# Norm gains spread by TensorE instead of loaded, two weight slabs outside the ring, and a rare path's loads on another queue, in a two-layer encoder with 32 experts

## The chip, the cores and the metric

One Trainium2 chip; the kernel runs on one of its cores. The metric is device time in microseconds (us), the median of several runs. Five engines work side by side, each from its own list of instructions: TensorE (PE; its weight loads stand in the profile as PEld), VectorE (DVE), ScalarE (ACT), GpSimd (POOL) and SyncE (SP). They wait for each other, and for transfers, on semaphores. Transfers (DMA) are issued from an engine's list and then run by themselves.

## What is computed

256 tokens of 1024 numbers pass two layers. In each, a mixer (pooling, a recurrent scan in two directions, attention) is followed by a norm, and this by a mixture of 32 experts and a second norm:

```python
x = layer_norm(DEEPNORM_ALPHA * x + y, ln1_g[l], ln1_b[l])      # y: the mixer's output
...
x = layer_norm(DEEPNORM_ALPHA * x + m, ln2_g[l], ln2_b[l])      # m: the experts' output
...
def layer_norm(x, g, b):
    xf = x.astype(jnp.float32)
    mu = jnp.mean(xf, -1, keepdims=True)
    var = jnp.mean(jnp.square(xf - mu), -1, keepdims=True)
    return ((xf - mu) * lax.rsqrt(var + LN_EPS) * g + b).astype(x.dtype)
...
    def expert_block(args):
        xb, e = args
        h = jax.nn.silu(xb @ w_gate[e]) * (xb @ w_up[e])
        return h @ w_down[e]
```

Each token goes to two experts of one group of eight; gain and bias of each norm are rows of 1024 numbers.

## The kernel before, in words

**Weights.** The experts' weights of a layer are 192 slabs of 128x2048 fp32 (1 MB each), in an order that the host lays out: 8 groups (NQ) of 4 experts, and of each group 8 slabs for gate, 8 for up, 8 for down. SP loads them in this order into a ring of 22 slabs (`slab()`, `RING`, `FLIGHT`); the name of the tile is `w`, that of the source `in_e_w`. The generator `loads` (line 1036) issues one load each time it is advanced (line 1039). 22 are issued ahead of the first group, while the mixer's end and the routing still run. Then `w(n)` takes the oldest slab and issues the next load, which waits until the matmuls of the slab that lay in its place are done. SP's loads go over eight lanes, each with a semaphore (DMAHW0 to DMAHW7), so that eight are out at a time and a ninth waits for the first of them.

**A group.** `experts` loops over the groups q. `gate_up` runs matmuls of gate (`pg`), then up (`pu`), a slab at a time; `between(n)` puts other work behind slab n. `hid_t` transposes the hidden rows (`pht`), `down` runs slabs 16 to 23 (`py`), ACT copies the result (`y`), and `combine` multiplies it with the one-hot matrix that scatters rows back to tokens (`pc`), which DVE adds to `xr`. The rows of the next group are gathered with a one-hot matrix `OH` by matmuls (`xg`); ACT and DVE apply gain and bias of the norm to them from columns (`lnc`), with the channel on the partition. A gathered place holds CH = 32 rows an expert.

**The norm rows.** The residual `xr` needs gain and bias along the row, the same on every partition. `ln_load` (line 1027) loads them with four broadcast transfers of 128x512 (256 KB each, line 1031): ahead of group 0 for the first norm, and after group 6 for the second. With the first, `gates` computes `xr` from the normed x in group 0 (lines 1177 to 1179): eight DVE instructions of 128x512, then two on ACT for the factor alpha. With the second, the layer's last norm is done. In the last layer `scaled` (lines 1440 to 1453) divides it between DVE and POOL, in unequal parts of the columns, and four transfers store the result.

**A path that is not taken.** Behind group 1 (`OVQ`) `overflow` (line 1303) tests whether an expert got more than 32 rows. All engines read the count (line 1304) and branch (line 1305); with these inputs the path is not taken. Within it weights are loaded once more, a quarter slab at a time (`ow`), from ACT's queue (line 1317).

**Order of the work.** The instructions stand on each engine in the order in which the code issues them. SBUF buffers of tag "r" (`s2`, nine of 128x512) and `x8` (two of 128x2x1024: one holds x, the other `x1T`, the transposed tokens for the router, and then `xr`) and eight PSUM banks (tag "r" five, `bank`; tag "c" three, `bankc`) are given out in that order too.

Of the kernel before, what the change touches and what calls it, by code (L numbers as in the profile page):

```python
# [22 lines left out]
NQ = NE // 4  # L23
ALPHA = float((2 * DEPTH) ** 0.25)
# [29 lines left out]
START = 9  # L54
OVQ = 1
FLIGHT = 22
LN_COLS0 = 704
LN_COLS = 832
VARIANT = [0, 1, 1, 0]
LOX = [0, 0, 0, 0]  # L60
PRE = 2
# [5 lines left out]

@with_exitstack
def tile_encoder(ctx: ExitStack, tc: tile.TileContext, x_tok, x_t, w_a0, w_a1, w_b0, w_b1, w_o,
                 cols, ln_rows, consts, rcnt, e_w, out):  # L70
    nc = tc.nc
    V, A, G, PE = nc.vector, nc.scalar, nc.gpsimd, nc.tensor
    PSUM = bass.MemoryType.PSUM
# [8 lines left out]
    def x8(name):  # L82
        return xp.tile([128, 2, D], F32, name=name, tag="x8", bufs=2)
# [16 lines left out]
    def slab(dt=F32):  # L100
        return wp.tile([128, 2048], dt, name="w", tag="w", bufs=RING)
# [30 lines left out]
    P = load_cols(0, E)  # L132
# [3 lines left out]
    x = x8("x")  # L136
# [3 lines left out]
    ident = kc[:, K_ID:K_ID + 128]  # L140
# [17 lines left out]
    slot = cp.tile([128, 2, NE], F32, name="slot")  # L158
# [3 lines left out]
    lnc = cp.tile([128, 392], F32, name="lnc")  # L162
# [46 lines left out]
    def s2(shape, name):  # L209
        return mp.tile(shape, F32, name=name, tag="r", bufs=RB)  # L210
# [812 lines left out]

        return [lambda i=i: put(i, 0, fin[0][i]) for i in range(2)], [second(i) for i in range(2)]

    def ln_load(l, n, one=False):
        gb = []
        t_ = slab() if one else None
        for m in range(4):
            b = t_[:, 512 * m:512 * m + 512] if one else s2([128, 512], "lnr")  # L1030
            nc.sync.dma_start(out=b, in_=ln_rows[l, n + m // 2:n + m // 2 + 1, 512 * (m % 2):512 * (m % 2) + 512].to_broadcast([128, 512]))
            gb.append(b)
        return gb

    def loads(l):
        for q in range(NQ):
            for n in range(24):
                t_ = slab()
                nc.sync.dma_start(out=t_, in_=e_w[l, q, n])
                yield t_.rearrange("p (a n) -> p a n", a=4)  # L1040

    def route_all(l, xh, wo_tail):
        gb = ln_load(l, 0)


        mask = tiny([128, 2, NE], "mask")
        iota32 = iota[:, 0:32]
# [1 line left out]
        xk = [xh[:, i].rearrange("p (c k) -> p k c", k=8) for i in range(2)]  # L1049
# [87 lines left out]
        mv0 = ln_rstd(st[0])  # L1137
# [8 lines left out]
        mv1 = ln_rstd(st[1])  # L1146
# [16 lines left out]
        xr = x8("xr")  # L1163

        def exps():
            next(r0)
# [2 lines left out]
        def gates():  # L1169
            for r in (r0, r1):  # L1170
                for _ in r:
                    pass
            yield
            for i in range(2):
                for h in range(2):
                    sl = (slice(None), i, slice(512 * h, 512 * h + 512))
                    V.tensor_tensor(xr[sl], xh[sl], gb[h], op=OP.mult)
                    V.tensor_tensor(xr[sl], xr[sl], gb[2 + h], op=OP.add)
                A.mul(xr[:, i], xr[:, i], ALPHA)

        def count():
            cm = tiny([128, 1], "cm")
# [3 lines left out]
            V.tensor_reduce(cnf, pcm[0:1, 0:128], axis=AX.X, op=OP.max)  # L1186
            V.tensor_copy(cnt, cnf)

        return xr, (oh0, banks), exps, gates, count

    def gather_half(ps, x1k, oh, i):
        for k in range(8):
# [16 lines left out]
    def experts(l, x1, xr, oh0, exps, gates, count, wts, feed):  # L1209

        x1k = x1.rearrange("p i (c k) -> p i k c", k=8)

# [27 lines left out]
        def gated(oh, gts):  # L1240
            V.tensor_tensor(oh, oh, gts.rearrange("p i (a s) -> p i a s", s=1).to_broadcast([128, 2, 4, CH]), op=OP.mult)
# [101 lines left out]
        xg = []  # L1343
        late_half(0)
        oh, done = oh0[0], None
        for q in range(NQ):
            def w(n):
                t_ = wts.pop(0)
                wts.extend(v_ for v_ in (next(feed, None),) if v_ is not None)
                return lambda a: t_[:, a]  # L1350

            more = q + 1 < NQ
            cut_ = q == OVQ
            if q:
                gated(oh, four(gate, q))
            nxt, oht, steps = [None], [], None

            def step(n):
                for _ in range(n):
                    nxt[0] = next(steps, nxt[0])  # L1360

            def between(n):
                nonlocal steps
                if q == 0 and n == 1:
                    late_half(1)
                    exps()
                    A.preload_act_table_set(SETS_SILU)
                    more_ = gates()
                    next(more_)
# [43 lines left out]
            if cut_:  # L1413
# [23 lines left out]
        mv0 = ln_rstd(st[0])  # L1437
        put(1, 1)
        if last:
            def scaled(i, mv, n):  # L1440
                for e, lo, hi in ((V, 0, n), (G, n, 1024)):
                    if e is G:
                        o_ = xr[:, i, lo:hi]
                        G.tensor_scalar(o_, o_, mv[:, 0:1], mv[:, 3:4], op0=OP.subtract, op1=OP.mult)  # L1444
                        G.tensor_tensor(o_, o_, gb[1][:, lo - 512:hi - 512], op=OP.mult)  # L1445
                        G.tensor_tensor(o_, o_, gb[3][:, lo - 512:hi - 512], op=OP.add)  # L1446
                    else:
                        for m, (c, op0, op1) in enumerate(((0, OP.subtract, OP.mult), (3, OP.mult, OP.add))):
# [53 lines left out]
    resid = iter(())  # L1502
    for l in range(DEPTH):
        wo_tail = mixer(l, P, x, *slabs[:2], *block, resid)
        feed = loads(l)
        wts = [next(feed) for _ in range(FLIGHT)]
        xr, oh0, exps, gates, count = route_all(l, x, wo_tail)
        x, slabs, P, block, resid = experts(l, x, xr, oh0, exps, gates, count, wts, feed)
# [43 lines left out]
def _layout(inp):  # L1552
# [7 lines left out]
    rw = 256  # L1560
# [52 lines left out]
    d["ln_rows"] = np.ascontiguousarray(np.stack([g["ln1_g"], g["ln1_b"], g["ln2_g"], g["ln2_b"]], 1))  # L1613
# [23 lines left out]
```

## Time and profile before

| | |
|---|---|
| median of 3 runs | 1278.93 us (1277.48 to 1283.57) |
| the profiled execution | 1281.9 us, its span 1280.1 us |
| mean granted TensorE clock | 0.871 of full speed |
| busy share of the span | PE 77%, DVE 26%, ACT 19%, POOL 7% |
| bytes moved | 438.67 MB, 343 GB/s over the span |
| chain that ended last | 24% loads of w from in_e_w, all else 1% and less |

Slices of equal length across the page tell where the stretches lie: the mixers are those in which little is moved (37 GB/s in the third slice, 9 GB/s in the 22nd), the experts those in which some 420 GB/s are moved. The experts of the first layer run from about 181 to 626 us, those of the second from about 821 to 1264 us. A share of busy time is an average over these; what an edit is worth has to be read in its stretch.

### The profile page before, as it was taken

The numbers are of one execution on the slowest core, as the hardware profiler recorded it, in microseconds if no ns is written. First come the engines' busy times: TensorE is split into PE (matmuls) and PEld (weight loads), VectorE is DVE, ScalarE is ACT, GpSimd is POOL, SyncE is SP. The second block draws the span as 40 slices with busy tenths as digits, with TensorE's granted clock in tenths as the row PEclk, the third lists the DMA queues.
The fourth block names the chain that finished last, engine by engine and source line by source line (L and its number), as shares of the span: only waits on it lengthen the run. The fifth ranks groups of instructions, "written<-read, shape, count | busy, mean of one in ns | idle before, by whom it ended". The sixth has DMA issues, their size and how long they took to land. (4 is left out here: it accounts for less than half of the span.)

```text
span 1280.1 us, 18020 instructions
## 1 busy us (share of the span) xinstructions
PE 985.9 (77%) x7571; PEld 480.6 (38%) x7571; DVE 335.9 (26%) x774; ACT 239.2 (19%) x554; POOL 94.0 (7%) x137
## 2 busy tenths in 40 slices
PE   8988998933997777776698979989239977777753
PEld 7755763220441212221286657632214422223100
DVE  5937632110100001010368286411001000010103
ACT  5326422001110101010252353220011101010000
POOL 1143000000000000000101451000000000000002
PEclk9979999965998888886799789999669988888887
DMA  9413789998999999999940227999989999999994
GB/s 373 165 37 131 307 327 418 420 418 331 420 419 419 420 420 420 420 419 420 417 170 9 89 79 320 365 420 420 419 330 420 419 420 420 419 420 420 419 420 188
DMA packets 63452, 438.67 MB, mean 343 GB/s; under 512 B 7040, under 2 KB 7296, under 8 KB 11520
## 3 DMA queue, kind: packets, MB, share of 16 engines
q1 hardware_dynamic: 62784, 436.61, 83.1%
q8 instruction: 64, 1.05, 0.3%
q10 hardware_dynamic: 576, 0.79, 0.2%
q14 instruction: 28, 0.23, 0.0%
HBM read 436.32 MB, written 1.05 MB: 342 GB/s over the span
## 5 line engine op out<-in xcount | busy, mean ns | idle before, releaser
L172 PE MATMUL pg<-w,xg 128*32 128x512 f32 x1024 | 143.4, 658 | 120.3 <-ACT xg L1230 73.1
L172 PE MATMUL pu<-w,xg 128*32 128x512 f32 x1024 | 157.0, 700 | 39.2 <-DMA w<-in_e_w_dram 39.1
L172 PE MATMUL py<-w,hT 128*32 128x512 f32 x1024 | 146.0, 697 | 53.4 <-DMA w<-in_e_w_dram 42.4
L1261 DVE TENSOR_TENSOR h<-h,pu 128x512 f32<-128x512 f32 x16 | 11.0, 688 | 422.5 <-PE pu L172 218.3
L172 PEld LDWEIGHTS pg<-w,xg 128*32 128x32 f32 x1024 | 25.3, 114 | 215.8 <-DMA w<-in_e_w_dram 87.2
L1230 ACT ACTIVATE xg<-xg,lnc 128x128 f32<-128x128 f32 x112 | 41.8, 457 | 326.5 <-PE xg L168 219.6
L1293 DVE TENSOR_TENSOR xr<-xr,pc 128x512 f32<-128x512 f32 x56 | 38.5, 688 | 242.2 <-PE pc L172 242.2
L168 PEld LDWEIGHTS xg<-OH,xr 128*128 128x128 f32 x256 | 65.0, 331 | 61.9 <-issue 55.5
L168 PEld LDWEIGHTS xg<-OH,x 128*128 128x128 f32 x256 | 65.0, 331 | 59.4 <-issue 53.0
L172 PEld LDWEIGHTS py<-w,hT 128*32 128x32 f32 x1024 | 29.1, 117 | 154.1 <-DMA w<-in_e_w_dram 83.4
L168 PE MATMUL xg<-OH,xr 128*128 128x128 f32 x256 | 75.7, 433 | 12.0 <-DVE OH L1201 4.0
L168 PE MATMUL xg<-OH,x 128*128 128x128 f32 x256 | 75.6, 429 | 11.0 <-PEq L1305 4.1
L172 PE MATMUL pc<-y,OHT 128*128 128x512 f32 x128 | 70.0, 641 | 1.4 <-ACT y L1285 1.4
L1285 ACT COPY y<-py 128x512 f32<-128x512 f32 x32 | 18.7, 585 | 242.8 <-PE py L172 242.8
L231 POOL TENSOR_TENSOR w<-w 128x512 fp32r<-128x512 f32 (+1 forms) x20 | 25.2, 1265 | 497.4 <-ACT w L230 497.4
L172 PEld LDWEIGHTS pu<-w,xg 128*32 128x32 f32 x1024 | 23.6, 116 | 97.7 <-DMA w<-in_e_w_dram 80.5
L269 PE MATMUL wo<-w 128*128 128x512 f32 x192 | 46.5, 398 | 0.0
L196 POOL TENSOR_TENSOR lnmv<-lnmv,eps 128x1 f32<-128x1 f32 x8 | 4.8, 602 | 524.5 <-DVE lnmv L195 524.5
L172 PEld LDWEIGHTS pc<-y,OHT 128*128 128x128 f32 x128 | 20.1, 190 | 54.4 <-issue 46.0
L269 PEld LDWEIGHTS wo<-w 128*128 128x128 f32 x192 | 35.6, 188 | 9.1 <-issue 1.6
L230 ACT CAST w<-w 128x512 fp32r<-128x512 f32 (+1 forms) x64 | 36.6, 602 | 8.8 <-DMA w<-in_w_a_dram 4.8
L168 PE MATMUL pq<-w 128*128 128x512 f32 x64 | 38.0, 740 | 0.0
(328 smaller groups left out, 1064.8 us busy)
## 6 DMA issues: line engine op xcount, KB each, us to landing
w<-in_e_w_dram SPq DMA_DIRECT2D x384, 1024.0 KB, 19.9
w<-in_w_b_dram SPq DMA_DIRECT2D x8, 1024.0 KB, 18.7
w<-in_w_o_dram SPq DMA_DIRECT2D x8, 1024.0 KB, 19.9
w<-in_w_a_dram SPq DMA_DIRECT2D x4, 1024.0 KB, 13.5
lnr<-in_ln_rows_dram SPq DMA_DIRECT2D x12, 256.0 KB, 14.5
w<-in_w_a_dram SPq DMA_DIRECT2D x4, 448.0 KB, 6.3
w<-in_w_a_dram SPq DMA_DIRECT2D x2, 896.0 KB, 12.4
w<-in_cols_dram SPq DMA_DIRECT2D x2, 790.0 KB, 10.5
```

The costliest lines, as they stand in the source:

```text
L168: PE.matmul(ps, lhsT=lhsT, rhs=rhs, start=start, stop=True, skip_group_check=True)
L172: PE.matmul(ps, lhsT=lhsT, rhs=rhs, start=start, stop=stop)
L196: G.tensor_tensor(mv[:, 3:4], mv[:, 2:3], eps[:, 4:5], op=OP.pow)
L230: A.copy(hi, src)
L231: (V, G)[LOW[m]].tensor_tensor(lo, src, hi.bitcast(F32), op=OP.subtract)
L269: PE.matmul(ps, lhsT=l_[a], rhs=r_[b], start=first and n == 0, stop=last, skip_group_check=True)
L1230: A.activation(t_[:, k], ps[:, k], AF.Identity, scale=lnc["g1"][:, m:m + 1], bias=lnc["b1"][:, m:m + 1])
L1261: V.tensor_mul(h_, h_, ps_u)
L1285: A.copy(y_, py)
L1293: V.tensor_add(o_, o_, ps)
```

## The change

It has five parts.

1. The input `ln_rows` and `ln_load` go, and with them four sets of four row loads. `ln_cols` makes half a row set with four matmuls: the column of gain or bias (`lnc`), broadcast along the free dimension, is the stationary operand, the identity the moving one, so that a PSUM bank holds 4 x 128 values, the same on each partition. The channel order of x is c*8+k, so the instructions that use it see x through `by_k`, with a step of 8 elements.
2. In group 0 `scaled` replaces the lines 1174 to 1179: three sets of four matmuls after slab 4 (`lng`, `lnb`, `lng`), one after slab 10 (`lnb`), and eight DVE instructions (scalar_tensor_tensor, 128x4x128) with alpha in them. The one-hot of the next group is made after slab 2 instead of slab 6.
3. In group 7 `early(1)`, behind slab 17, makes the second set: four groups of matmuls with four ACT copies into a slab (first layer), or three that stay in PSUM, and a fourth at the end (last layer). `normed` does the last norm on DVE alone and stores in three transfers.
4. `Feed` replaces `loads`. Slabs 2 and 3 of the first group lie outside the ring: slab 3 as four quarters (`rw`) in the four buffers that the rows had, slab 2 (`xw`) in the buffer of `x1T`, once the routing is done with it. The first release of a ring place past them is the one of slab 4.
5. The general path's `ow` loads are issued from GpSimd's queue.

```diff
-    def ln_load(l, n, one=False):
...
-            nc.sync.dma_start(out=b, in_=ln_rows[l, n + m // 2:n + m // 2 + 1, 512 * (m % 2):512 * (m % 2) + 512].to_broadcast([128, 512]))
...
+    def ln_cols(ps, name, h):
+        ps = ps.rearrange("p (k t) -> p k t", k=4)
+        for k in range(4):
+            m = 4 * h + k
+            mm(ps[:, k], lnc[name][:, m:m + 1].to_broadcast([128, 128]), ident)
+        return ps
+
+    def by_k(t_):
+        return t_.rearrange("p (c k) -> p k c", k=8)
+    X8, R4 = 2, 3
+    class Feed:
...
+        def ring(self):
+            while self.at in (X8, R4):
+                self.at += 1
+            if self.at < 24 * NQ:
+                self.put(self.at, slab())
+                self.at += 1
+        def quarters(self):
+            t_ = [s2([128, 512], "rw") for _ in range(4)]
+            for a in range(4):
+                nc.sync.dma_start(out=t_[a], in_=self.src(R4)[:, 512 * a:512 * a + 512])
+            self.got[R4] = lambda a: t_[a]
+        def wide(self):
+            self.put(X8, x8("xw").rearrange("p i d -> p (i d)"))
+        def take(self, n):
+            t_ = self.got.pop(n)
+            if n not in (X8, R4):
+                self.ring()
+            return t_
...
-                    V.tensor_tensor(xr[sl], xh[sl], gb[h], op=OP.mult)
-                    V.tensor_tensor(xr[sl], xr[sl], gb[2 + h], op=OP.add)
-                A.mul(xr[:, i], xr[:, i], ALPHA)
+        def scaled(xr):
+            a, b = [[by_k(t_[:, i]) for i in range(2)] for t_ in (xh, xr)]
+            def mul(h, ps):
...
+                    V.scalar_tensor_tensor(b[i][sl], a[i][sl], ALPHA, ps, op0=OP.mult, op1=OP.mult)
+            def add(h, ps):
...
+                    V.scalar_tensor_tensor(b[i][sl], ps, ALPHA, b[i][sl], op0=OP.mult, op1=OP.add)
+            ps = [ln_cols(bankc("lng"), "g1", 0), ln_cols(bankc("lnb"), "b1", 0), ln_cols(bankc("lng"), "g1", 1)]
+            mul(0, ps[0])
+            yield
+            add(0, ps[1])
+            mul(1, ps[2])
+            yield
+            add(1, ln_cols(bankc("lnb"), "b1", 1))
...
-                                nc.scalar.dma_start(out=t_, in_=v_[:, 512 * a:512 * a + 512])
+                                nc.gpsimd.dma_start(out=t_, in_=v_[:, 512 * a:512 * a + 512])
...
+                if q == 0 and n == 4:
+                    xr = x8("xr")
+                    more_ = scaled(xr)
+                if q == 0 and n in (4, 7, 10):
                     next(more_, None)
...
-                elif n == 6 and more and not cut_:
+                elif n == 6 and q and more and not cut_:
...
+                elif n == 2 and not q and more and not cut_:
...
+                if n == 1:
+                    if l + 1 == DEPTH:
+                        by.extend(ln_cols(bankc("lnr"), name, h) for name, h in (("g2", 0), ("g2", 1), ("b2", 0)))
+                    else:
+                        t_ = slab()
+                        gb.extend(t_[:, 512 * m:512 * m + 512] for m in range(4))
+                        for m, name in enumerate(("g2", "b2")):
+                            for h in range(2):
+                                A.copy(by_k(t_[:, 1024 * m:1024 * m + 1024])[:, 4 * h:4 * h + 4], ln_cols(bankc("lnr"), name, h))
...
-            if q == NQ - 2:
-                gb = ln_load(l, 2, l + 1 < DEPTH)
...
+            by.append(ln_cols(bank("lnr"), "b2", 1))
+            def normed(i, mv, parts):
+                xk = by_k(xr[:, i])
+                for n, (lo, hi) in enumerate(parts):
+                    for m, (c, op0, op1) in enumerate(((0, OP.subtract, OP.mult), (3, OP.mult, OP.add))):
+                        for h in range(2):
+                            o_ = xk[:, 4 * h:4 * h + 4, lo:hi]
+                            V.scalar_tensor_tensor(o_, o_, mv[:, c:c + 1], by[2 * m + h][:, :, lo:hi], op0=op0, op1=op1)
+                    (nc.scalar if n % 2 else nc.sync).dma_start(out=out[:, i, 8 * lo:8 * hi], in_=xr[:, i, 8 * lo:8 * hi])
...
+            normed(0, mv0, ((0, 128),))
+            normed(1, mv1, ((0, 64), (64, 128)))
...
+        feed = Feed(l)
+        for _ in range(FLIGHT):
+            feed.ring()
+        feed.quarters()
+        rest = route_all(l, x, wo_tail)
+        feed.wide()
```

**SP at the branch of the first layer.** Rows between two slabs' loads, with the semaphores that each waits for; line 1305 is line 1346 after, the slab load's line 1039 is 1045. Before:

```order
L1039 DMA w<-in_e_w_dram 128x2048 [waits DMAHW7_49,PE_49]
L1304 TENSOR_LOAD cnt [waits DVE_49]
L1304 ISA x2
L1305 COMPARE_AND_BRANCH
L1310 COMPARE_AND_BRANCH
L1310 UNCONDITIONAL_BRANCH [waits DMAHW0_49,DMAHW1_49,DMAHW2_49,DMAHW3_49,DMAHW4_49,DMAHW5_49,DMAHW6_49,DMAHW7_49]
...
L1305 UNCONDITIONAL_BRANCH [waits DMAHW0_49,DMAHW1_49,DMAHW2_49,DMAHW3_49,DMAHW4_49,DMAHW5_49,DMAHW6_49,DMAHW7_49]
L1039 DMA w<-in_e_w_dram 128x2048 [waits DMAHW0_49,PE_49]
```

After:

```order
L1045 DMA w<-in_e_w_dram 128x2048 [waits DMAHW6_49,PE_49]
L1345 TENSOR_LOAD cnt [waits DVE_49]
L1345 ISA x2
L1346 COMPARE_AND_BRANCH
L1351 COMPARE_AND_BRANCH
L1351 UNCONDITIONAL_BRANCH
...
L1346 UNCONDITIONAL_BRANCH
L1045 DMA w<-in_e_w_dram 128x2048 [waits DMAHW7_49,PE_49]
```

The rows of the branch that waited for the eight lanes, ahead of the load that follows, have no wait.

**PE in group 0 of the first layer**, from the first gate slabs on (four rows a slab; `xg<-OH,x` in the third row of before and after is the second half of the first gather). Before:

```order
L168 MATMUL xg<-OH,x 128x128 x4
L172 MATMUL pg<-w,xg 32x512 x8
L168 MATMUL xg<-OH,x 128x128 x4
L172 MATMUL pg<-w,xg 32x512 x24
L1246 MATMUL oht<-kc,OH 128x128 x2
L172 MATMUL pu<-w,xg 32x512 x4
L168 MATMUL xg<-OH,x 128x128
L172 MATMUL pu<-w,xg 32x512 x4
L168 MATMUL xg<-OH,x 128x128
L172 MATMUL pu<-w,xg 32x512 x4
```

After:

```order
L166 MATMUL xg<-OH,x 128x128 x4
L170 MATMUL pg<-w,xg 32x512 x8
L166 MATMUL xg<-OH,x 128x128 x4
L170 MATMUL pg<-xw,xg 32x512 x4
L170 MATMUL pg<-rw,xg 32x512 x4
L170 MATMUL pg<-w,xg 32x512 x4
L170 MATMUL lng<-kc,lnc 128x128 x4
L170 MATMUL lnb<-kc,lnc 128x128 x4
L170 MATMUL lng<-kc,lnc 128x128 x4
L170 MATMUL pg<-w,xg 32x512 x12
L1287 MATMUL oht<-kc,OH 128x128 x2
L170 MATMUL pu<-w,xg 32x512 x4
```

Three sets of four matmuls stand behind the fifth slab (`w` after `xw` and `rw`), ahead of the last three of gate.

**DVE in group 0 of the first layer**: the one-hot of the next group is `OH<-kc,slot`. Before:

```order
L1241 TENSOR_TENSOR OH<-OH,gate 128x256
L1177 TENSOR_TENSOR xr<-x,lnr 128x512
L1178 TENSOR_TENSOR xr<-xr,lnr 128x512
...
L1178 TENSOR_TENSOR xr<-xr,lnr 128x512
L1201 TENSOR_TENSOR OH<-kc,slot 128x256
L1261 TENSOR_TENSOR h<-h,pu 128x512
```

After:

```order
L1282 TENSOR_TENSOR OH<-OH,gate 128x256
L1242 TENSOR_TENSOR OH<-kc,slot 128x256
L1207 SCALAR_TENSOR_TENSOR xr<-x,lng 128x4x128 x2
L1212 SCALAR_TENSOR_TENSOR xr<-lnb,xr 128x4x128 x2
L1207 SCALAR_TENSOR_TENSOR xr<-x,lng 128x4x128 x2
L1212 SCALAR_TENSOR_TENSOR xr<-lnb,xr 128x4x128 x2
L1302 TENSOR_TENSOR h<-h,pu 128x512
```

The one-hot stood behind the xr instructions and stands ahead of them now.

## Rows read from the trace of the kernel before

**Rows 1.** Chain of work that ended last, second layer: start us, us, what.

```profile
969.20 19.90 DMA w<-in_e_w_dram
```

**Rows 2.** SP's own waits, whole span: us in total, times, longest us.

```profile
SPq L1039 <- DMA w<-in_e_w_dram: 584.0, 282, 3.2
SPq L1305 <- SPq L1305: 37.5, 14, 6.4
```

**Rows 3.** Busy time by stretch: PE, PEld, DVE, ACT, POOL, granted clock, DMA share, GB/s.

```profile
180.00:185.00 5.00, 4.45 (x22) 1.67 (x21) 0.82 (x2) 0.91 (x2) 0.00 (x0) 0.66 0.09 23
176.00:240.00 64.00, 57.97 (x377) 24.76 (x380) 15.01 (x40) 11.98 (x27) 0.00 (x0) 0.95 0.92 373
300.00:340.00 40.00, 29.38 (x186) 13.14 (x190) 1.71 (x3) 6.87 (x18) 0.00 (x0) 0.82 0.85 349
314.00:600.00 286.00, 227.43 (x1296) 75.99 (x1288) 23.66 (x39) 26.69 (x62) 0.00 (x0) 0.89 1.01 419
800.00:870.00 70.00, 62.89 (x391) 34.24 (x389) 22.23 (x77) 14.79 (x31) 0.55 (x1) 0.95 0.97 395
940.00:980.00 40.00, 30.76 (x202) 13.61 (x206) 1.71 (x3) 6.87 (x18) 0.00 (x0) 0.84 0.85 349
```

**Rows 4.** Line 1305: SP's events (x count, ns, first and last start), and who waited.

```profile
L1305 SPq EVENT_SEMAPHORE  x16: 17/17/17, 291.8 to 947.8; - x16
  ACT xg L1230: 106.9, 2
```

**Rows 5.** Timeline of SP, 286 to 290 and 310 to 313: start us, us, instruction.

```profile
286.83 2.82 SPq L1039 DMA_DIRECT2D w<-in_e_w_dram  x2
...
311.83 0.34 SPq L1039 DMA_DIRECT2D w<-in_e_w_dram  x1
```

**Rows 6.** Timeline of PE, 250 to 290 and 286 to 316; [idle before <-releaser].

```profile
268.48 4.44 PE L168 MATMUL xg<-OH,x 128*128 128x128 f32 x18 [1.64 <-issue]
...
309.84 6.35 PE L172 MATMUL pg<-w,xg 128*32 128x512 f32 x36 [36.92 <-ACT xg L1230]
```

**Rows 7.** Timeline of SP, 183 to 184.5 and 190 to 193.3.

```profile
183.81 0.33 SPq L1039 DMA_DIRECT2D w<-in_e_w_dram  x1
...
190.07 2.90 SPq L1039 DMA_DIRECT2D w<-in_e_w_dram  x4
```

**Rows 8.** Timeline of PE, last group of each layer.

```profile
604.29 1.12 PE L1268 MATMUL pht<-kc,h 128*128 128x128 f32 x4 [0.88 <-DVE h L1261]
...
624.12 1.52 PE L172 MATMUL py<-w,hT 128*32 128x512 f32 x8 [0.57 <-DMA w<-in_e_w_dram]
...
1242.03 0.75 PE L1268 MATMUL pht<-kc,h 128*128 128x128 f32 x4 [0.88 <-DVE h L1261]
...
1252.55 1.93 PE L172 MATMUL py<-w,hT 128*32 128x512 f32 x8 [0.57 <-DMA w<-in_e_w_dram]
1255.10 1.77 PE L172 MATMUL py<-w,hT 128*32 128x512 f32 x8 [0.61 <-DMA w<-in_e_w_dram]
...
1260.21 1.06 PE L172 MATMUL py<-w,hT 128*32 128x512 f32 x8 [1.43 <-DMA w<-in_e_w_dram]
```

**Rows 9.** Timeline of PE, 176 to 200: six gate slabs of group 0.

```profile
187.23 5.36 PE L172 MATMUL pg<-w,xg 128*32 128x512 f32 x48
```

**Rows 10.** Timeline of DVE, 184 to 202: the instruction ahead of the xr ones.

```profile
191.78 0.43 DVE L1241 TENSOR_TENSOR OH<-OH,gate 128x256 f32<-128x256 f32 x1
```

**Rows 11.** DVE by line and shape: xcount | busy us, mean ns | idle before.

```profile
L699 DVE TENSOR_TENSOR w<-w 128x512 f32<-128x512 f32 x4 | 4.3, 1064 | 0.1
L1451 DVE SCALAR_TENSOR_TENSOR xr<-xr,lnmv,lnr 128x512 f32<-128x512 f32 x4 | 3.0, 742 | 0.0
L677 DVE TENSOR_TENSOR w<-lo 128x256 f32<-128x256 f32 x2 | 1.2, 594 | 0.1
```

**Rows 12.** Timeline of all engines, 1262 to 1281: the last norm.

```profile
1269.15 5.16 DVE L1451 SCALAR_TENSOR_TENSOR xr<-xr,lnmv,lnr 128x512 f32<-128x512 f32 x8
...
1276.77 0.59 POOL L1446 TENSOR_TENSOR xr<-xr,lnr 128x192 f32<-128x192 f32 x1
```

More of the change, by code (lines that the diff above doesn't have):

```diff
@@ L56 @@
 FLIGHT = 22
-LN_COLS0 = 704
-LN_COLS = 832
 VARIANT = [0, 1, 1, 0]
@@ L69, in tile_encoder @@
 def tile_encoder(ctx: ExitStack, tc: tile.TileContext, x_tok, x_t, w_a0, w_a1, w_b0, w_b1, w_o,
-                 cols, ln_rows, consts, rcnt, e_w, out):
+                 cols, consts, rcnt, e_w, out):
     nc = tc.nc
@@ L1024, in mixer, with __init__, src, put @@
         return [lambda i=i: put(i, 0, fin[0][i]) for i in range(2)], [second(i) for i in range(2)]
-    def ln_load(l, n, one=False):
[L1027 to L1030, printed above, removed]
-            nc.sync.dma_start(out=b, in_=ln_rows[l, n + m // 2:n + m // 2 + 1, 512 * (m % 2):512 * (m % 2) + 512].to_broadcast([128, 512]))
[L1032 to L1040, printed above, removed]
+    def ln_cols(ps, name, h):
[8 more added lines that the diff above has]
+    class Feed:
+        def __init__(self, l):
+            self.l, self.got, self.at = l, {}, 0
+        def src(self, n):
+            return e_w[self.l, n // 24, n % 24]
+        def put(self, n, t_):
+            nc.sync.dma_start(out=t_, in_=self.src(n))
+            v_ = t_.rearrange("p (a n) -> p a n", a=4)
+            self.got[n] = lambda a: v_[:, a]
+        def ring(self):
[16 more added lines that the diff above has]
+            return t_
     def route_all(l, xh, wo_tail):
-        gb = ln_load(l, 0)
         mask = tiny([128, 2, NE], "mask")
@@ L1162, in route_all @@
         one_hot_half(oh0, 1)
-        xr = x8("xr")
         def exps():
@@ L1172, in gates @@
                     pass
-            yield
-            for i in range(2):
-                for h in range(2):
-                    sl = (slice(None), i, slice(512 * h, 512 * h + 512))
-                    V.tensor_tensor(xr[sl], xh[sl], gb[h], op=OP.mult)
-                    V.tensor_tensor(xr[sl], xr[sl], gb[2 + h], op=OP.add)
-                A.mul(xr[:, i], xr[:, i], ALPHA)
+        def scaled(xr):
+            a, b = [[by_k(t_[:, i]) for i in range(2)] for t_ in (xh, xr)]
+            def mul(h, ps):
+                for i in range(2):
+                    sl = (slice(None), slice(4 * h, 4 * h + 4))
+                    V.scalar_tensor_tensor(b[i][sl], a[i][sl], ALPHA, ps, op0=OP.mult, op1=OP.mult)
+            def add(h, ps):
+                for i in range(2):
+                    sl = (slice(None), slice(4 * h, 4 * h + 4))
+                    V.scalar_tensor_tensor(b[i][sl], ps, ALPHA, b[i][sl], op0=OP.mult, op1=OP.add)
+            ps = [ln_cols(bankc("lng"), "g1", 0), ln_cols(bankc("lnb"), "b1", 0), ln_cols(bankc("lng"), "g1", 1)]
+            mul(0, ps[0])
+            yield
+            add(0, ps[1])
+            mul(1, ps[2])
+            yield
+            add(1, ln_cols(bankc("lnb"), "b1", 1))
         def count():
@@ L1187, in count @@
             V.tensor_copy(cnt, cnf)
-        return xr, (oh0, banks), exps, gates, count
+        return (oh0, banks), exps, gates, scaled, count
     def gather_half(ps, x1k, oh, i):
@@ L1207, in one_hot_half, with experts @@
                         op=OP.is_equal)
-    def experts(l, x1, xr, oh0, exps, gates, count, wts, feed):
+    def experts(l, x1, oh0, exps, gates, scaled, count, feed):
         x1k = x1.rearrange("p i (c k) -> p i k c", k=8)
@@ L1341, in late_half @@
             xg.append(t_)
-        xg = []
+        xg, xr, gb, by = [], None, [], []
         late_half(0)
@@ L1347, in w @@
             def w(n):
-                t_ = wts.pop(0)
-                wts.extend(v_ for v_ in (next(feed, None),) if v_ is not None)
-                return lambda a: t_[:, a]
+                return feed.take(24 * q + n)
             more = q + 1 < NQ
@@ L1355, in experts @@
                 gated(oh, four(gate, q))
-            nxt, oht, steps = [None], [], None
+            nxt, oht, steps, more_ = [None], [], None, None
             def step(n):
@@ L1362, in between @@
             def between(n):
-                nonlocal steps
+                nonlocal steps, xr, more_
                 if q == 0 and n == 1:
@@ L1367, in between @@
                     A.preload_act_table_set(SETS_SILU)
-                    more_ = gates()
-                    next(more_)
+                    gates()
                     gated(oh, four(gate, q))
+                if q == 0 and n == 4:
+                    xr = x8("xr")
+                    more_ = scaled(xr)
+                if q == 0 and n in (4, 7, 10):
                     next(more_, None)
@@ L1375, in between @@
                     oht.append(slots_t(oh))
-                elif n == 6 and more and not cut_:
+                elif n == 6 and q and more and not cut_:
+                    ohn.append(one_hot(four(slot, q + 1)))
+                    steps = gather_steps(ohn[0])
+                elif n == 2 and not q and more and not cut_:
                     ohn.append(one_hot(four(slot, q + 1)))
@@ L1404, in early @@
             def early(n):
-                if q + 1 == NQ and n == 5:
+                if q + 1 < NQ:
+                    return
+                if n == 1:
[7 more added lines that the diff above has]
+                                A.copy(by_k(t_[:, 1024 * m:1024 * m + 1024])[:, 4 * h:4 * h + 4], ln_cols(bankc("lnr"), name, h))
+                if n == 5:
                     for i in range(2):
@@ L1504, in tile_encoder @@
         wo_tail = mixer(l, P, x, *slabs[:2], *block, resid)
[L1505 to L1508, printed above, removed]
+        feed = Feed(l)
[4 more added lines that the diff above has]
+        feed.wide()
+        x, slabs, P, block, resid = experts(l, x, *rest, feed)
 def _consts():
@@ L1612, in _layout @@
     d["cols"] = c
-    d["ln_rows"] = np.ascontiguousarray(np.stack([g["ln1_g"], g["ln1_b"], g["ln2_g"], g["ln2_b"]], 1))
     d["consts"], d["rcnt"] = _consts()
```

16 lines of the change are left out of this document (removed).

## The prediction

> **What bounds the kernel now.** I read the chain of work that ended last first. Through the experts of the second layer it is one load after another of `w` from `in_e_w`, 19.9 us from issue to landing [rows 1]: the stream of weight slabs sets the time. The queue's own waits say the same: SP's load line waited 584 us, 282 times, for an earlier load to land [rows 2]. Next I read the transfer rate by stretch [rows 3]. In the long middle of a layer it is 419 GB/s, so a slab of 1 MB (1048576 bytes) takes 2.50 us, and only what leaves the stream idle, or puts bytes into it that aren't slabs, is worth anything there. In three places of each layer the stream is not whole.
>
> (a) *The branch after group 1.* From 300 to 340 and from 940 to 980 the rate is 349. 40 x (419 - 349) / 419 = 6.7 us of stream are lost in each. SP itself stands in line 1305: 16 semaphore events, 37.5 us of waiting in both layers [rows 2, 4]. It issued its last slab before the branch at 289.3 (the second of the pair from 286.83 on) and the next at 311.83 [rows 5], so all eight loads that were out had landed before a ninth was asked for. PE had gathered group 2 by 268.48 + 4.44 = 272.9, but its first matmul came at 309.84, after 36.9 us for ACT's xg, which waited for that same SP line, 106.9 us in the two layers [rows 4, 6].
>
> (b) *The first group.* From 176 to 240 the rate is 373 (64 x 46 / 419 = 7.0 us lost), from 800 to 870 it is 395 (4.0 us). The stream is dry in the slice from 180 to 185, 23 GB/s [rows 3]: 22 slabs and the four row loads were issued long before, and the next slab goes out at 183.81, when PE gives the first one back [rows 7]. The 0.1 MB of that slice also tells that data flow about 1.2 us after an issue.
>
> (c) *The norm rows.* Each set of four loads is 4 x 256 KB, 1 MB of stream: 2.5 us. One set lies ahead of group 0, one in group 7: PE starts a slab there at 1255.10 and the next only at 1260.21, 5.1 us instead of 2.5 [rows 8].
>
> **The change, part by part**, against the profiled execution (1281.9 us; its span is 1280.1).
>
> *Weight loads of the general path from GpSimd's queue.* None of them runs. But the eight lane semaphores that they used from ACT's queue are those of SP's loads, and so SP waited for all eight lanes at the branch. In the changed order SP's branch rows have no such wait, and the lanes that ACT's xg waits for are GpSimd's own, which nothing uses. The test of the count, PE's own branch and the gather stay. PE is then back at 273. The first slab behind the branch needs the ring place of the first slab of group 2, which PE gives back at about 274; its lane is free 2.5 us after the last issue, at 291.8. So nothing else stops the stream. I take all of it: -6.7 twice, **-13.4 us**. What is late next is PE itself: from 255 to 273 it takes no slab, some seven of them (18 / 2.5) pile up, and it works them off at 0.9 us each (5.36 us for six [rows 9]) against 2.5 of the stream.
>
> *The second set of rows.* Its 2.5 us a layer leave the stream, but 16 matmuls (layer 1 of the two, with four ACT copies) or 12 (the last layer) go onto PE after slab 17 of group 7. The nearest matmul of this shape is pht: four rows, 0.75 us in the last layer and 1.12 in the first [rows 8]; one group of four fp32 matmuls is eight rows, 1.5 us, or 2.2 by the slower row. Last layer: slab 21 of the group starts at 1255.10, so slab 17, four steps of 2.5 ahead, at 1245.1, and ends at 1246.1; three groups end at 1250.6; slabs 18 to 21 at some 1.5 us (rows of 1.06 to 1.93 [rows 8]) end at 1256.6, the two pc with 2.0 at 1258.6, slab 23 at 1261.6, where before ended 2.5 + 1.1 after the start at 1260.21, at 1263.8, and the stream alone would allow 1261.3. So -2.2. First layer: slab 23 starts at 624.12 and ends at 625.6 [rows 8]; slab 18 stands five steps of 2.5 and the 2.5 of the rows ahead of it, at 609.1, and PE is free there. Four groups, 6.0, six slabs at 1.3 and the two pc, 2.0, end at 624.9: -0.7. Together **-2.9** (both ends: -5.0 if PE hides all; +5 if every row takes the slow value, for then PE and not the stream ends the layer).
>
> *First group.* Before, what is lost of useful stream in layer 0 is 7.0 + 2.5 for the rows = 9.5. After, 24 slabs instead of 22 are asked for before PE must give one back, so the stream runs dry 2.5 us later, at about 182. But slabs 2 and 3 now release nothing: the order of PE is slabs 0, 1, late half, 2, 3, 4, then three groups lng, lnb, lng. Slab 24 goes out at 183.81 as before, 25 behind it, 26 at 190.07 (the place of the fifth issue of before, for the fifth slab [rows 7]). Then the third group needs the PSUM bank of the first: three banks of that tag, one holds pg. It waits for two multiplications on DVE, which is free at 192.2 [rows 10] and has the next one-hot first (0.4): 192.6 + 2 x 1.0 + 1.5 for the group + 0.9 for slab 5 = 197.0 is the next issue. Idle: 182.0 to 185.0, 190.0 to 191.3, 193.8 to 198.2, 8.7 us; and the ramps of a stream of single slabs, which made 7.0 of a gap of some 5.5 before, add 1: 9.7. So the two slabs and the rows gained are given back in the wait at slab 4: **0** for each layer (together -1.4 with the matmul groups at 1.3, to +3.1 with groups at 2.2 and 1.4 a multiplication).
>
> *The new DVE forms.* They read x and write xr with a step of 8 elements, 32 bytes. Contiguous, this instruction costs 0.742 for 128x512. Two strided rows are near: line 677 writes 128x256 with a step of 64 bytes in 0.594, 1.38 times the 0.43 of a contiguous 128x256, and line 699 takes 1.064 for 128x512, 1.43 times the 0.742 [rows 10, 11]. I take 1.0, a factor F of 1.35, by line 677, whose pattern is the nearer one; the ends are 1 (a stride that costs nothing; no row suggests a gain) and 2. [...]
>
> *Tail.* DVE starts the last norm at 1269.15, POOL ends its part at 1276.77 + 0.59, and the span ends 2.7 later, at 1280.1 [rows 12]. Now DVE alone does 4 of 128x512 and 8 of 128x256: 1269.15 + 4 x 1.0 + 8 x 0.57 = 1277.7 (0.57 from the 0.43 of a contiguous 128x256 [rows 10], times 1.35). The last store is larger than before's, 128x512 instead of 128x192: I take 3.0 to the end, 1280.7. **+0.6** (-1.5 contiguous, +5 at twice). The last ln group on PE lies beside bn_stats and costs nothing unless DVE is earlier than now.
>
> Sum: -13.4 - 2.9 + 0 + 0.6 = -15.7, so 1266.2 for a profiled execution. The median of the runs shown is 1278.93, 3.0 under the profiled one: 1278.93 - 15.7 = **1263.2**, rounded 1263. Its own range: low all terms good, -13.4 - 5.0 - 1.4 - 1.5 = -21.3, 1257.6; high, with half of the bad ends together, some 1270.
>
> **Rivals.**
>
> *B, the stream still stops at the branch* (0.07). Another wait takes the place: the change doesn't do what it says. For: four engines and SP still test the count there, and POOL, which now carries the loads, has a wait for its own lanes; against: POOL was through this branch long before the others in before. Price: the 13.4 come back, 1276.6.
>
> *C, the first group pays* (0.12). If the third group finds its bank (the multiplications done by 192.6) the next issue is 195.0 instead of 197.0, 2 us a layer: 1259. Against: DVE is busy with the gates until 192.2.
>
> *D, strided DVE costs twice* (0.10). The place is line 1207 and 1212 in each first group and the last norm. One unit of F is 4 x 0.74 on the path at slabs 4 to 8 of each layer and 4 x 0.74 + 8 x 0.42 = 6.3 in the tail: 12.3 us. F = 2 instead of 1.35: +8.0, 1271.
>
> *E, slower* (0.03). The same mechanism, far out: with F over 1.35 + 15.7 / 12.3 = 2.6 the gain is gone, with F over 3.2 it is slower by over 0.5%; at F = 3.5, 1263.2 + 26.4 = 1289.6. For: PE can't start pu before DVE has freed the bank, so every DVE microsecond there stops the ring. Against: the strided rows stand at 1.43 at most.
>
> The rest, 0.68, is the forecast.
>
> **How the numbers follow.** A measurement of this kernel can tell about 0.5%, 6.4 us, from no change, so "faster" is below 1272.5. The forecast, C and most of D (0.07) are: 0.87. "Same" is B and the rest of D: 0.09. "Slower" is E and what I haven't thought of: 0.04. The range: 1256 (C with a good tail) to 1271 (D) leaves out B, E, half of D and the ends of the forecast: about 0.2.
>
> **What would show each step.** Right: no semaphore events of SP at the branch line, no gap near 289 to 313 and 928 to 952, a GB/s row on the page without its two dips inside the long stretches of 420, PE's first matmul of group 2 near 274. Slab 26 issued near 190 and slab 27 near 197, the third lng group waiting for DVE line 1207. PE in group 7 without a step of 5.1. DVE's 128x4x128 near 1.0 and a tail of 17 us behind the last py. It is wrong if SP still stands at the branch, if a strided DVE instruction is over 1.5, or if PE's ln groups are over 2.2 and the last slab of a group 7 waits for PE and not for its load.

## The result, and the profile after

The changed kernel takes 1263.33 us (median of 4 runs, 1261.39 to 1266.53), the kernel before in the same comparison 1279.56. The ratio is 0.9883, 95% interval [0.9861, 0.9905]: 16.2 us less. Forecast were 15.7 us less and 1263. The profiled execution took 1262.4 us, its span 1260.3.

Transfer rate by stretch in the changed kernel (columns as in [rows 3]):

```profile
176.00:240.00 64.00, 59.28 (x375) 27.95 (x378) 17.96 (x40) 9.83 (x25) 0.00 (x0) 0.93 0.86 345
195.00:200.00 5.00, 5.00 (x32) 2.24 (x32) 3.78 (x4) 0.00 (x0) 0.00 (x0) 0.66 0.10 16
300.00:340.00 40.00, 31.22 (x158) 6.22 (x161) 4.11 (x7) 3.65 (x8) 0.00 (x0) 0.74 1.01 419
```

300 to 340 was 349 and is 419: the stop at the branch is gone. 176 to 240 was 373 and is 345, with a new empty stretch from 195 to 200. The branch line of the changed kernel is 1346; of SP it holds no event any more, only the branch, and PE goes on with group 2 as soon as the gather is done (against 309.84 in [rows 6]):

```profile
L1346 POOLq EVENT_SEMAPHORE  x8: 17/43/43, 226.9 to 850.6; - x8
L1346 POOLq INC_SWDGE_SEM  x2: 168/172/177, 227.2 to 850.7; - x2
L1346 SPq COMPARE_BRANCH  x2: 50/52/53, 291.0 to 914.7; - x2
```

```profile
265.29 7.86 PE L166 MATMUL xg<-OH,x 128*128 128x128 f32 x32 [4.13 <-PEq L1346]
273.08 3.21 PE L170 MATMUL pg<-w,xg 128*32 128x512 f32 x28
```

PE in group 0 (timeline): the third set of four matmuls waits for DVE. Under it, in SP's timeline, is the load that follows, slab 27 at 198.62:

```profile
191.15 1.06 PE L170 MATMUL lnb<-kc,lnc 128*128 128x128 f32 x8
194.85 1.84 PE L170 MATMUL lng<-kc,lnc 128*128 128x128 f32 x8 [2.65 <-DVE xr L1207]
```

```profile
198.62 0.33 SPq L1045 DMA_DIRECT2D w<-in_e_w_dram  x1
```

PE in group 7 of the first layer (matmuls `py` of slabs 21, 22 and 23, as in [rows 8] for the last layer). Before, 5.1 us lay between the starts of slabs 21 and 22, the place of the row loads:

```profile
616.49 1.06 PE L172 MATMUL py<-w,hT 128*32 128x512 f32 x8 [1.48 <-DMA w<-in_e_w_dram]
...
621.63 1.93 PE L172 MATMUL py<-w,hT 128*32 128x512 f32 x8 [2.16 <-DMA w<-in_e_w_dram]
```

After, the sixteen matmuls take 4.67 us, 2.9 us lie between slabs 21 and 22, and slab 23, 2.1 us later, is waited for as a load:

```profile
602.90 4.67 PE L170 MATMUL lnr<-kc,lnc 128*128 128x128 f32 x32
...
610.56 1.06 PE L170 MATMUL py<-w,hT 128*32 128x512 f32 x8 [0.28 <-DMA w<-in_e_w_dram]
...
613.47 1.06 PE L170 MATMUL py<-w,hT 128*32 128x512 f32 x8
615.54 1.07 PE L170 MATMUL py<-w,hT 128*32 128x512 f32 x8 [1.00 <-DMA w<-in_e_w_dram]
```

The new instructions by line and shape (columns as in [rows 11]):

```profile
L1207 DVE SCALAR_TENSOR_TENSOR xr<-x,lng 128x512 f32<-128x512 f32 x4 | 4.1, 1078 | 0.1
L1502 DVE SCALAR_TENSOR_TENSOR xr<-xr,lnmv,lnr 128x512 f32<-128x512 f32 x4 | 4.2, 1118 | 0.0
L1502 DVE SCALAR_TENSOR_TENSOR xr<-xr,lnmv,lnr 128x256 f32<-128x256 f32 x8 | 4.7, 662 | 0.0
L1460 ACT COPY w<-lnr 128x512 f32<-128x512 f32 x4 | 3.9, 1123 | 27.5 <-PE lnr L170 27.5
L1326 ACT COPY y<-py 128x512 f32<-128x512 f32 x32 | 18.8, 586 | 230.8 <-PE py L170 230.8
```

**Where the time went.** I cut every profiled span at five points: PE's first gate matmul of each layer, SP's compare at the branch, the end of the last py of each layer. The stretches between them, in us, for all kernels (e1 to e8 are the experiments below):

| kernel | layer 1: start to branch | branch to end | mixer | layer 2: start to branch | branch to end | tail |
|---|---|---|---|---|---|---|
| before | 108.7 | 335.1 | 195.7 | 107.5 | 335.0 | 16.3 |
| after | 108.8 | 325.6 | 191.1 | 107.0 | 327.2 | 18.4 |
| e1, queue alone | 107.9 | 330.1 | 190.8 | 107.9 | 329.4 | 17.4 |
| e2, ACT's queue | 110.1 | 332.7 | 192.1 | 108.5 | 332.7 | 17.4 |
| e3, no slabs outside | 110.8 | 325.5 | 192.6 | 107.6 | 327.3 | 17.3 |
| e4, sets late | 104.6 | 325.6 | 194.7 | 103.3 | 327.0 | 17.9 |
| e5, tail copied | 108.7 | 325.6 | 190.9 | 108.1 | 326.2 | 17.9 |
| e6, late and tail | 103.1 | 326.9 | 194.1 | 103.0 | 327.1 | 17.0 |
| e7, late, no slabs outside | 108.1 | 325.6 | 191.6 | 107.4 | 326.8 | 17.9 |
| e8, mul twice | 111.7 | 325.6 | 194.1 | 112.0 | 326.6 | 18.4 |

From before to after the expert stretches give 9.5 - 0.1 in the first layer and 0.5 + 7.8 in the second, the tail takes 2.1 back, the first gate matmul is 0.4 later, and 4.6 come from the mixer between them, whose own instructions were not changed.

Each row of the table is one profile, so the table also tells how far the same code differs. The starts with the same code there lie up to 1.5 us apart (after, e2 and e5; e4 and e6). The first layer from branch to end repeats within 0.1 us in six profiles of the same code (after, e3, e4, e5, e7, e8), with e6 1.3 above. The tail took 16.3 and 17.4 with the code of before (before, e1), and 17.3 to 18.4 with that of after (after, e2, e3, e4, e7, e8).

### The profile page after: what moved, and what is told of

Same layout as the page of the kernel before. It is cut to its first block, busy times and chain, and to the rows that moved or that the text cites. A ratio compares the mean times of both kernels' runs of the same rounds, so it can differ in the third digit from the quotient of the medians.

```text
span 1260.3 us, 18267 instructions
## 1 busy us (share of the span) xinstructions
PE 1016.7 (81%) x7699; PEld 492.9 (39%) x7699; DVE 345.6 (27%) x778; ACT 239.4 (19%) x554; POOL 87.1 (7%) x131
## 5 line engine op out<-in xcount | busy, mean ns | idle before, releaser
L170 PE MATMUL pu<-w,xg 128*32 128x512 f32 x1024 | 161.0, 717 | 55.5 <-DMA w<-in_e_w_dram 55.2
L170 PE MATMUL py<-w,hT 128*32 128x512 f32 x1024 | 149.0, 699 | 62.0 <-DMA w<-in_e_w_dram 51.0
L170 PE MATMUL pc<-y,OHT 128*128 128x512 f32 x128 | 74.5, 679 | 1.4 <-ACT y L1326 1.4
## 6 DMA issues: line engine op xcount, KB each, us to landing
w<-in_w_a_dram SPq DMA_DIRECT2D x4, 1024.0 KB, 15.2
```

Of the source, the lines that this page charges most:

```text
L170: PE.matmul(ps, lhsT=lhsT, rhs=rhs, start=start, stop=stop)
```

## The experiments

The changed kernel was timed once, with the result. The kernel before was timed again beside e1 to e4 (1279.02 us) and beside e5 to e8 (1279.22), against 1279.56 there, so the medians can be compared across the three. Each interval below reaches some 3 to 4 us to either side.

**e1, the queue alone**: the kernel before with one word changed.

```diff
-                                nc.scalar.dma_start(out=t_, in_=v_[:, 512 * a:512 * a + 512])
+                                nc.gpsimd.dma_start(out=t_, in_=v_[:, 512 * a:512 * a + 512])
```

Expected: 

> The kernel before, with nothing changed but the queue of the general path's weight loads (GpSimd's instead of ACT's). If the stop of the stream at the branch comes from the eight lanes that ACT's loads share with SP's, it goes here alone: no events of SP at the branch line, PE's first matmul of group 2 near 273, and 13.4 us less than the kernel before (1279.6 - 13.4 = 1266). If the stop has another cause (the branch itself, PE's own time in it), or goes only together with the row loads, the time stays within 3 us of the kernel before.

Measured: 1266.84 us against 1279.02, ratio 0.9908 [0.9876, 0.9939]: 12.2 us less. All that SP has left at the branch line, the rate by stretch, and PE's restart in its timeline:

```profile
L1305 SPq COMPARE_BRANCH  x2: 50/52/53, 290.7 to 919.5; - x2
```

```profile
300.00:340.00 40.00, 28.31 (x157) 5.54 (x159) 4.11 (x7) 3.65 (x8) 0.00 (x0) 0.83 1.01 419
```

```profile
274.19 4.50 PE L172 MATMUL pg<-w,xg 128*32 128x512 f32 x40
```

The stop came from the lanes, and that one word removes it. It takes away two waits at once, that of SP, which issues the loads, and that of ACT's xg, which held PE; no run parts them.

**e2, the changed kernel with the loads on ACT's queue**, the same edit the other way.

Expected: 

> The changed kernel with the general path's loads back on ACT's queue, all else as changed. The same theory: both stops come back, 12 to 14 us slower than the changed kernel (1275 to 1278), SP's wait for eight lanes at the branch line again some 18 us a layer. The rival, that the other parts carry the gain: 1263 to 1267.

Measured: 1274.73, ratio to before 0.9974 [0.9953, 0.9996]; 11.4 us slower than the changed kernel, just under the 12 to 14 that were expected. SP's waits and the rate show the old stop, and ACT's xg waits 107.6 us for it in the two layers, as before:

```profile
SPq L1346 <- SPq L1346: 37.5, 15, 3.7
```

```profile
  ACT xg L1271: 107.6, 2
```

```profile
300.00:340.00 40.00, 27.69 (x178) 12.71 (x182) 1.71 (x3) 6.89 (x18) 0.00 (x0) 0.82 0.83 335
```

So of some 16 us the queue is worth 11 to 12 by the medians, all else together 4 to 5.

**e3, slabs 2 and 3 in the ring** (22 ahead):

```diff
-    X8, R4 = 2, 3
+    X8, R4 = -1, -2
...
-        feed.quarters()
         rest = route_all(l, x, wo_tail)
-        feed.wide()
```

Expected: 

> The changed kernel with slabs 2 and 3 of each layer in the ring like all others (22 ahead, no quarters, none in the x8 buffer). Theory: the two slabs are given back for the most part in the wait of the third matmul group at slab 4, because they release no place of the ring: the stream then runs dry at 177 instead of 182, but has five slabs instead of three to move until PE goes on near 198; 1 to 3 us slower over both layers (1264 to 1266), with the branch of the first layer 0.5 to 1.5 us later against PE's start. Rival: the two slabs are worth their full 5 us of stream in each layer: 10 us slower, 1273.

Measured: 1264.35, ratio to before 0.9891 [0.986, 0.9923]; 1.0 us over the changed kernel, less than the two intervals are wide. The start of the layers is 2.0 and 0.6 us longer, hardly more than the same code differs. 10 us are excluded: the two slabs outside the ring bring little in this kernel, 1 us by the medians and 2.6 by the two starts.

**e4, the four sets one at a time after slabs 8, 10, 12 and 14:**

```diff
-            ps = [ln_cols(bankc("lng"), "g1", 0), ln_cols(bankc("lnb"), "b1", 0), ln_cols(bankc("lng"), "g1", 1)]
-            mul(0, ps[0])
-            yield
-            add(0, ps[1])
-            mul(1, ps[2])
-            yield
-            add(1, ln_cols(bankc("lnb"), "b1", 1))
+            for h in range(2):
+                mul(h, ln_cols(bankc("lng"), "g1", h))
+                yield
+                add(h, ln_cols(bankc("lnb"), "b1", h))
+                yield
...
-                if q == 0 and n in (4, 7, 10):
+                if q == 0 and n in (8, 10, 12, 14):
```

Expected: 

> The changed kernel with the four matmul groups of the first norm rows one at a time after slabs 8, 10, 12 and 14 instead of three after slab 4 and one after slab 10, each followed by its two DVE instructions. Theory: the idle stretch of the stream from about 195 to 200 us (and its counterpart in the second layer) comes from PE's wait for DVE after slab 4, so slab 27 is asked for near 191 instead of 198.6, the stretch goes, and the kernel gains 4 to 5 us a layer: 1254 to 1256. Rival: the stream is short at the start anyhow (too few places free) or the wait moves to up's groups: within 2 us of the changed kernel.

Measured: 1255.05, ratio to before 0.9807 [0.9774, 0.9841]: 8.3 us under the changed kernel, 4.2 and 3.7 of them in the two starts. The stretch from 195 to 200 is full (windows), and slabs 26 to 28 go out from 191.16 on (timeline of SP):

```profile
195.00:200.00 5.00, 5.00 (x39) 3.08 (x36) 2.09 (x2) 0.00 (x0) 0.00 (x0) 1.00 1.01 419
```

```profile
191.16 2.04 SPq L1045 DMA_DIRECT2D w<-in_e_w_dram  x3
```

The gap came from what stood on PE between slabs 4 and 5: three groups, 4.06 us by the timeline, and the wait of 2.65 for DVE. This run takes both away at once, so it doesn't tell the wait from the groups; e8 changes the wait alone.

**e5, the last norm as before**: `early(1)` copies the rows by ACT in both layers, and the tail uses the old division between DVE and POOL.

```diff
-                    if l + 1 == DEPTH:
-                        by.extend(ln_cols(bankc("lnr"), name, h) for name, h in (("g2", 0), ("g2", 1), ("b2", 0)))
-                    else:
...
-            normed(0, mv0, ((0, 128),))
-            normed(1, mv1, ((0, 64), (64, 128)))
+            halves(0, mv0, LN_COLS0)
+            halves(1, mv1, LN_COLS)
```

Expected: 

> The changed kernel with the last norm of the last layer as before: the rows are made by the same matmuls but copied by ACT into a slab (as the first layer does), and read with step 1 by DVE and POOL in the old shares. Theory (the 32-byte step costs DVE some 1.5 times): DVE's instructions of the tail fall from 1.118 to 0.74 for 128x512, their sum from 8.8 to some 5.2, and the time from the last py to the end from 18.4 to some 16.5 to 17.5: 1 to 2 us faster than the changed kernel (1261 to 1262.5), which the median alone can hardly show. Rival, that the PSUM operand and not the step makes them slow: 0.74 as well, for there is none left here; it is told apart by the pc additions, which have a PSUM operand with step 1 and stand at 0.69.

Measured: 1260.56, ratio to before 0.9859 [0.9824, 0.9893]; 2.8 us under the changed kernel, within the noise of both. DVE's part of the tail is 5.16 us instead of 8.84 (timeline), but POOL ends it, at 1255.85, and the tail is 17.9 instead of 18.4, longer than the 16.5 to 17.5 expected:

```profile
1247.65 5.16 DVE L1504 SCALAR_TENSOR_TENSOR xr<-xr,lnmv,w 128x512 f32<-128x512 f32 x8
...
1255.26 0.59 POOL L1499 TENSOR_TENSOR xr<-xr,w 128x192 f32<-128x192 f32 x1
```

By line and shape, the additions that read a PSUM operand with step 1 and the instruction of the last norm with step 1, both of this run; then, of the changed kernel, the same kind of instruction with step 1 and a PSUM operand (`wo`):

```profile
L1448 DVE TENSOR_TENSOR xr<-xr,pc 128x512 f32<-128x512 f32 x8 | 5.4, 680 | 34.3 <-PE pc L172 34.3
L1504 DVE SCALAR_TENSOR_TENSOR xr<-xr,lnmv,w 128x512 f32<-128x512 f32 x4 | 3.0, 742 | 0.0
```

```profile
L1013 DVE SCALAR_TENSOR_TENSOR x<-x,wo 128x512 f32<-128x512 f32 x4 | 2.7, 682 | 4.5 <-PE wo L267 4.5
```

With step 1 a PSUM operand adds nothing here (0.680 and 0.682), so it is the step that makes 0.742 into 1.118. Of the 3.7 us that DVE saves, the tail shows 0.5, which is less than it differs with the same code: POOL, which the changed kernel doesn't use there, ends the norm instead.

**e6, e4 and e5 together.**

Expected: 

> The late matmul groups (after slabs 8, 10, 12, 14) and the tail of the run before together. The two don't touch: 1255.1 less 1 to 2 us, 1253 to 1254.5.

Measured: 1253.18, ratio to before 0.9788 [0.9762, 0.9814]; 10.2 us under the changed kernel, as expected and the fastest of the study; the tail's share of it, 1.9 against e4, is within the noise.

**e7, e4 without the slabs outside the ring.**

Expected: 

> The late matmul groups, with slabs 2 and 3 in the ring (22 ahead). Theory: where PE no longer waits at slab 4, each slab more ahead is worth its 2.5 us of stream, less what the ramp takes: 3.5 to 4.5 us a layer slower than with the slabs outside, 1262 to 1264. Rival, that the two slabs are worth the 1 us that they were with the wait: 1255 to 1257.

Measured: 1260.91, ratio to before 0.9848 [0.9818, 0.9879]; 5.9 us over e4, a little less than expected in the time, and 3.5 and 4.1 in the two starts, as expected. Together with e3: the same two slabs are worth 1.0 us (2.6 in the starts) with the sets and the wait at slab 4, and 5.9 (7.6) without them.

**e8, the first pair of multiplications done twice:**

```diff
             mul(0, ps[0])
+            mul(0, ps[0])
             yield
```

Expected: 

> The changed kernel with the first pair of multiplications after slab 4 done twice in each layer, two more DVE instructions of 1.08 us (the result is the same). Theory: PE's third group waits for them and the ring for PE, so 2.1 us later in each layer, the branch 2 us later against PE's start, 1267.5 (1266.5 to 1268.5). Rival, that DVE there is covered by slabs already landed: 1263 to 1264.

Measured: 1269.78, ratio to before 0.9924 [0.9896, 0.9952]; 6.5 us over the changed kernel, more than the 4.2 expected. The two instructions lengthen PE's wait to 4.59 in both layers, from 2.65 in the first and 1.35 in the second. Timeline of PE in e8's first layer (the changed kernel's stands in the section on the result), then in the second layer, of the changed kernel and of e8:

```profile
195.18 2.05 PE L170 MATMUL lng<-kc,lnc 128*128 128x128 f32 x8 [4.59 <-DVE xr L1207]
197.16 4.32 PE L170 MATMUL pg<-w,xg 128*32 128x512 f32 x24
```

```profile
820.30 1.13 PE L170 MATMUL lng<-kc,lnc 128*128 128x128 f32 x8 [1.35 <-DVE xr L1207]
821.36 2.78 PE L170 MATMUL pg<-w,xg 128*32 128x512 f32 x24
```

```profile
826.60 2.05 PE L170 MATMUL lng<-kc,lnc 128*128 128x128 f32 x8 [4.59 <-DVE xr L1207]
828.58 4.34 PE L170 MATMUL pg<-w,xg 128*32 128x512 f32 x24
```

Busy time in the stretch from the third set on: e8 in the first layer (195 to 200 stands above for the changed kernel), then the second layer of both:

```profile
195.00:200.00 5.00, 4.82 (x24) 2.57 (x28) 4.12 (x5) 0.00 (x0) 0.00 (x0) 0.50 0.01 3
```

```profile
820.30:825.00 4.70, 4.70 (x42) 1.97 (x42) 3.96 (x4) 0.45 (x2) 0.00 (x0) 1.00 0.46 159
```

```profile
826.60:832.00 5.40, 5.40 (x28) 2.65 (x32) 3.92 (x4) 0.00 (x0) 0.00 (x0) 0.52 0.02 3
```

DVE time at this place lengthens both starts in full, and a price that I had left out comes with it: behind the longer wait the granted clock was lower. In the second layer it was 0.52 instead of 1.00, and the same work took 0.9 + 1.6 longer. The wait is 3.2 longer there, but 1.2 of this is no loss: PE came to the sets 8.0 us after the layer's first gate matmul and not 9.2 (timeline). The 2.0 of DVE and the 2.5 of the clock make 4.5; the start of the layer is 5.0 longer. In the first layer the wait is 1.9 longer, the clock 0.50 instead of 0.66, the work 0.2 + 0.6 slower, 2.7 together (3.68 of the gate matmuls became 4.32, timeline); the start is 2.9 longer. (Starts of the same code differed by up to 1.5.) In these four places the clock behind the wait was 1.00, 0.66, 0.52 and 0.50 for waits of 1.35, 2.65, 4.59 and 4.59. In e3's first layer, behind a wait of 2.59, the third set took 1.13 and the gate matmuls 2.78 (timeline), as here at 1.00, so the length of the wait alone doesn't give the clock.

## Why the prediction was right, step by step

*The branch* (-13.4). Right in mechanism: e1 removes it alone and e2 brings it back alone. By the medians it is -12.2 and -11.4, by the stretches from branch to end -10.6 (5.0 + 5.6) and -12.6 (7.1 + 5.5); the intervals of the medians don't tell these from -13.4. The step took the stream that was idle, 6.7 a layer, as time at the end. In the first layer of e1 5.0 seem to be left of it, because the stretches don't carry the same bytes. First layer from branch to end, before, e1 and after (columns as in [rows 3]):

```profile
290.50:625.64 335.14, 248.47 (x1392) 80.39 (x1392) 27.70 (x45) 30.17 (x71) 0.00 (x0) 0.85 0.99 411
290.70:620.82 330.12, 242.51 (x1272) 73.20 (x1268) 27.70 (x45) 26.32 (x61) 0.00 (x0) 0.84 1.01 419
291.00:616.61 325.61, 245.31 (x1300) 77.55 (x1300) 27.71 (x45) 30.23 (x65) 0.00 (x0) 0.84 1.01 420
```

Time and rate make 137.7 MB before and 138.3 in e1, 1.4 us of stream more, which is most of the 1.7 that seem to be missing (half a GB/s of rounding is 0.4 us). In the second layer, where 1.1 are missing, the last py ran slower in e1, 1.94 us at a granted clock of 0.50 instead of 1.07 at 1.00, which is 0.9 of them. PE in its timeline and the last 2 us of the stretch, before and e1:

```profile
1262.70 1.07 PE L172 MATMUL py<-w,hT 128*32 128x512 f32 x8 [1.42 <-DMA w<-in_e_w_dram]
```

```profile
1261.77:1263.77 2.00, 1.07 (x8) 0.16 (x8) 0.00 (x0) 0.00 (x0) 0.00 (x0) 1.00 0.03 12
```

```profile
1246.91 1.94 PE L172 MATMUL py<-w,hT 128*32 128x512 f32 x8 [1.42 <-DMA w<-in_e_w_dram]
```

```profile
1246.85:1248.85 2.00, 1.94 (x8) 0.20 (x8) 0.00 (x0) 0.00 (x0) 0.00 (x0) 0.50 0.00 0
```

*The second set of rows* (-2.9). Larger: -2.4 and -2.3 from before to e2, and -4.5 and -2.2 from e1 to after, both with the same branch. No run takes these rows out alone; these are remainders. The last layer came as I had it (-2.2); in the first (-0.7) I mis-sized PE's part: a group of four matmuls took 1.17 us (4.67 for four), where I took 1.5 by pht, so PE was not late and the last slab was waited for as a load. That the first layer gives 4.5 without the stop is the other side of the bytes above: 138.3 against 136.8 MB is 3.6 us of stream, of which the rows are 2.5.

*The first group* (0). Right, by its own steps: +0.1 and -0.5 (e2 against before, with the same code in the starts as after: +1.4 and +1.0). The next load after the wait came 16.4 us after PE's start at 182.22, forecast 15.2 (197.0 from 181.81); DVE's pair took 2.04 where I had 2.0, the third set 1.84 where I had 1.5. e3, e4, e7 and e8 show the mechanism: the two slabs pay only where the stop at slab 4 goes. Rival C priced the removal of this wait at 2 us a layer; e4, which also takes the three groups away from there, is worth 4.

*DVE and the tail* (F = 1.35, +0.6). F is 1.118 / 0.742 = 1.51: with the step of 32 bytes the instruction took half as much again, not the twice of rival D, which was a bound that I had assumed and which no run shows. The rows before could have told: line 699 is a TENSOR_TENSOR, and I divided its 1.064 by the 0.742 of another instruction. Against the contiguous TENSOR_TENSOR of the same shape it is 1.54 times:

```profile
L1178 DVE TENSOR_TENSOR xr<-xr,lnr 128x512 f32<-128x512 f32 x8 | 5.5, 692 | 0.3
```

At 1.51 the tail formula gives 1269.15 + 4 x 1.118 + 8 x 0.662 + 3.0 = 1281.9, +1.8 instead of +0.6; measured +2.1 in the one pair of profiles. That the two agree is in part luck: DVE took 8.84 where the formula has 9.8, but began 0.6 later after the last py, and the end came 3.6 after DVE, not 3.0 (timeline). Over all profiles the tail has 16.8 as a mean with the code of before (two) and 17.9 with that of after (six), so +1.0 to +2.1 is what they support.

*The sum.* By the profiles the difference of the spans is 19.8, not 15.7, but 4.6 of it is the mixer, 195.7 in the one and 191.1 in the other, at a granted clock of 0.90 and 0.93. Its code is the same in all ten kernels and it took 190.8 to 195.7; e1, which is the kernel before with one word changed, took 190.8, so the 4.6 are none of the change's doing. Why it differs stays open. Without it the profiles give 15.2. The errors are -13.4 against some -12, -2.9 against some -5, +0.6 against +1 to +2, and cancel in part: that the sum came within 0.5 us of the medians' 16.2, whose interval goes from 12.2 to 17.8, is partly luck.

## What to carry to other kernels

Look at which queue a rarely taken path issues its loads from. Here they shared completion semaphores with the main stream, and the stream's queue waited for all eight where the path is skipped, though nothing of it runs; e1, which moves these loads alone, was 12.2 us faster. Before buying buffers to prefetch more, look for the first wait of the consumer, since it decides whether the buffers pay: two slabs were worth 1 us behind a wait and 6 without it. And spread side work on PE in pieces that never wait for the reader of their PSUM bank: in e8 a wait of 4.59 us instead of 2.65 and 1.35 cost its own length, and the granted clock behind it was 0.50 and 0.52 instead of 0.66 and 1.00.

## What the runs showed that I had not expected

- The step of 32 bytes cost ACT more than DVE: the copies that write with it took 1.123 us for 128x512, the contiguous copy of y 0.586, 1.9 times as much; for DVE's last norm it was 1.118 against 0.742, 1.5 times.
- Skipping the path on GpSimd's queue isn't free but hidden: four semaphore events and an INC_SWDGE_SEM of 0.17 us a layer on POOL, in the first at 227 us, 64 us before SP's branch.
- Unchanged code, the mixer of the second layer, differed by 4.9 us over the ten profiles, at mean granted clocks of 0.90 to 0.95, as much as some of the effects looked for here. The clock alone doesn't order them: 190.8 came at 0.91 (e1) and 192.6 at 0.94 (e3). The cut into stretches told these apart where spans could not.
